# Three chunks per layer of an MLP's second product as seven block products, with groups and chunks strictly alternating

## The chip, the cores and the metric

The kernel runs on one core of a Trainium2 chip. The metric is the device time of one execution in microseconds, taken as the median of several runs. The core's engines are TensorE (PE, with PEld for its weight loads), VectorE (DVE), ScalarE (ACT), GpSimd (POOL) and SyncE (SP, which issues the DMA transfers here).

## The reference

A decoder trunk of two layers over 512 tokens of width 1024. The mixers differ from layer to layer (spatial gating beside latent attention in layer 0, gated linear attention in layer 1); the change touches only the MLP, which is the same in both:

```python
def sqrelu_mlp(x, w1, w2):            # w1: 1024 x 4096, w2: 4096 x 1024, all float32
    return jnp.square(jax.nn.relu(x @ w1)) @ w2
...
        x = layer_norm(ALPHA * x + y, ln1_g[layer], ln1_b[layer])
        x = layer_norm(ALPHA * x + sqrelu_mlp(x, w_ff1[layer], w_ff2[layer]), ln2_g[layer], ln2_b[layer])
```

## The kernel before

**Precision.** Each float32 operand is split in two parts for the matmuls: a high part (`whi`, `hh`), which ACT makes by a cast, and a low part (`wlo`, `hl`), which DVE makes by subtracting the high part from the operand. A product is then three matmuls: high by high, low by high, high by low. So a weight piece of 128 x 1024 costs one DMA, one ACT cast and one DVE subtraction (`split`, lines 164 and 165).

**First product, by groups.** `ff` cuts the 4096 hidden columns into eight groups. Group g holds 256 columns from each half of the hidden dimension. Its operands are cut in 2 x 2 blocks: the transposed x into A11 to A22 (halves of the model dimension by halves of the tokens), w1 into B11 to B22, and the hidden result into the blocks C11, C12, C21, C22 (the first index is the token half, the second the hidden half). Group 0 multiplies the blocks plainly, in eight products. Groups 1 to 7 use seven: P1, P2, p3 to p7, whose operands are sums of blocks (s1 to s4 of x, kept for the whole layer, and t1 to t4 of w1, made on DVE by `sum1`, line 374). `product` runs the 24 matmuls of one product and then, by `step`, the DVE work for which it completes the inputs: V after p6, X after p5 and V, C22 after X and p7, C12 after p3, C11 after P2, C21 after p4. The list LATER sets the order of the seven. Each finished hidden block goes through `relu2`: ACT relu, ACT square, ACT cast to `hh`; the subtraction that makes `hl` is put on the list `late` and issued on DVE by the next `flush`, which stands ahead of each product.

**Second product, by chunks.** Chunk c multiplies the hidden blocks of group c by the rows of w2 that belong to them. In `ff2_half` one token tile t (128 tokens) and one half n of the 1024 output columns make a bank of 12 matmuls of 512 columns, after which DVE adds the bank onto XN (`add_half`, line 208). A chunk is eight such halves, 96 matmuls. Chunks 6 and 7 are multiplied together at the end, where the layer norm follows.

**Order.** `slots` lists products and halves in PE's order and `wseq` the weight pieces in the order of their use. Ahead of each slot `upto(n)` issues the loads of pieces up to six places beyond n, and the casts, sums and subtractions of the pieces up to n; for a group's product n grows with the group's number (three places ahead in group 1, six from group 4 on). PE and DVE run the MLP in the order in which the code issues. The slots of before are group 0, chunk 0, group 1, chunk 1, group 2, chunk 2, groups 3 and 4, chunk 3, group 5, chunk 4, group 6, chunk 5, group 7, chunks 6 and 7.

**Buffers.** Raw w2 pieces go round three buffers (tag `raw`), high and low parts of weights round eight each, hidden parts `hh` and `hl` round eight each. The PSUM banks of both products are dealt in turn from six.

## Time and profile before

| | |
|---|---|
| time, median of 3 runs | 1167.64 us (1166.27 to 1169.44) |
| the profiled execution | 1168.8 us, of which the trace spans 1167.1 us |
| PE, DVE, ACT busy | 98%, 71%, 44% of the span |
| mean granted TensorE clock | 0.997 |
| traffic | 111.68 MB by DMA, mean 96 GB/s |

An engine's busy share counts the time in which at least one of its instructions ran. A matmul's record is longer than the distance to the next matmul's start, since they are pipelined; the same holds to a lesser degree on DVE and ACT. For what a stretch costs, distances between starts are therefore read. [...]

### The profile page before, as it was taken

To read this page: it belongs to the slowest core of one execution; us is meant where nothing else is said; L and a number is where in the kernel's file an instruction comes from. 1 tells how busy PE (TensorE), PEld (TensorE's weight loads), DVE (VectorE), ACT (ScalarE), POOL (GpSimd) and SP (SyncE) were. 2 spreads that over 40 slices of the span, in tenths; PEclk is the share of its full clock that TensorE was granted. 3 is DMA by queue.
4 is the path that set the end of the run, shared out by engine and by line. 5 is a ranking of instruction groups with operands and counts; after the bars stand their busy time and mean duration, and the time that the engine had idled before them with its cause. 6 is when DMAs were issued, how large, how long until landed. Compare 5 with 4: busy or idle time off the path is not lost.

```text
span 1167.1 us, 17136 instructions
## 1 busy us (share of the span) xinstructions
PE 1142.6 (98%) x6888; PEld 996.6 (85%) x6888; DVE 827.2 (71%) x1562; ACT 516.1 (44%) x801; POOL 5.0 (0%) x13
## 2 busy tenths in 40 slices
PE   8999999999999999999999999999999999999997
PEld 8988788898889998998888888778997899889986
DVE  6745687786766767657758559898767577676655
ACT  5467462444343634533254433443544437345330
POOL 0000000000000000000000000000000000000000
PEclk9999999999999999999999999999999999999999
DMA  7413143133412342224235312212133224314121
GB/s 254 140 37 108 55 132 104 37 109 109 126 57 88 127 126 74 89 74 140 72 98 145 90 55 73 73 61 67 59 125 117 85 85 144 127 38 127 54 90 55
DMA packets 84207, 111.68 MB, mean 96 GB/s; under 512 B 6080, under 2 KB 53056, under 8 KB 84128
## 3 DMA queue, kind: packets, MB, share of 16 engines
q1 hardware_dynamic: 84128, 110.59, 30.1%
q8 instruction: 54, 0.88, 0.3%
q14 instruction: 25, 0.20, 0.1%
HBM read 108.47 MB, written 2.10 MB: 95 GB/s over the span
## 4 chain that ended last, share of the span: by engine, by line
PE 88%; DVE 7%; ACT 4%; DMA 0%; issue 0%; SPq 0%; DVEq 0%; ACTq 0%
PE f L451 23%; PE f L161 10%; PE f L159 10%; PE f L160 10%; PE vg L159 3%; PE vg L160 3%; PE vg L161 3%; PE op L159 2%; PE op L161 2%; PE op L160 2%; PE sc L836 1%; PE qk L159 1%; PE qk L160 1%; PE qk L161 1%; PE o L858 1%; PE pl L1117 1%
## 5 line engine op out<-in xcount | busy, mean ns | idle before, releaser
L161 PE MATMUL f<-whi,hl 128*128 128x512 f32 x448 | 178.0, 397 | 5.5 <-DVE hl L431 5.5
L159 PE MATMUL f<-whi,hh 128*128 128x512 f32 x448 | 177.9, 397 | 1.3 <-ACT hh L430 1.3
L164 ACT CAST whi<-cr 128x1024 fp32r<-128x1024 f32 x98 | 100.8, 1048 | 174.7 <-PE f L161 81.4
L160 PE MATMUL f<-wlo,hh 128*128 128x512 f32 x448 | 177.3, 396 | 0.0
L165 DVE TENSOR_TENSOR wlo<-cr,whi 128x1024 fp32r<-128x1024 f32 x98 | 119.2, 1220 | 23.0 <-ACT whi L164 23.0
L451 PE MATMUL f<-XH,wlo 128*128 128x256 f32 x448 | 125.9, 281 | 0.0
L451 PE MATMUL f<-XH,whi 128*128 128x256 f32 x448 | 125.8, 281 | 0.0
L451 PE MATMUL f<-XL,whi 128*128 128x256 f32 x448 | 125.8, 281 | 0.0
L161 PEld LDWEIGHTS f<-whi,hl 128*128 128x128 f32 x448 | 84.7, 189 | 27.8 <-DVE hl L431 8.1
L208 DVE SCALAR_TENSOR_TENSOR XN<-XN,f 128x512 f32<-128x512 f32 (+1 forms) x113 | 74.3, 678 | 43.9 <-PE f L161 43.1
L159 PEld LDWEIGHTS f<-whi,hh 128*128 128x128 f32 x448 | 84.7, 189 | 21.1 <-ACT hh L430 2.1
L160 PEld LDWEIGHTS f<-wlo,hh 128*128 128x128 f32 x448 | 84.8, 189 | 19.3
L451 PE MATMUL f<-sl,whi 128*128 128x256 f32 x336 | 94.5, 281 | 0.0
L451 PE MATMUL f<-sh,wlo 128*128 128x256 f32 x336 | 94.5, 281 | 0.0
L451 PE MATMUL f<-sh,whi 128*128 128x256 f32 x336 | 94.4, 281 | 0.0
L431 DVE TENSOR_TENSOR hl<-r,hh 128x512 fp32r<-128x512 f32 x64 | 44.1, 690 | 60.5 <-ACT hh L430 60.5
L451 PEld LDWEIGHTS f<-XL,whi 128*128 128x128 f32 x448 | 84.4, 188 | 0.5
L451 PEld LDWEIGHTS f<-XH,whi 128*128 128x128 f32 x448 | 84.4, 188 | 0.5
L451 PEld LDWEIGHTS f<-XH,wlo 128*128 128x128 f32 x448 | 84.4, 188 | 0.0
L164 ACT CAST whi<-raw 128x1024 fp32r<-128x1024 f32 x56 | 58.0, 1050 | 54.0 <-PE f L451 35.7
L137 ACT CAST whi<-raw 128x1024 fp32r<-128x1024 f32 (+3 forms) x61 | 60.2, 991 | 47.6 <-DMA raw<-in_w_in_odd 18.8
L138 DVE TENSOR_TENSOR wlo<-raw,whi 128x1024 fp32r<-128x1024 f32 (+3 forms) x61 | 69.7, 1148 | 14.6 <-ACT whi L137 14.3
(270 smaller groups left out, 2528.7 us busy)
## 6 DMA issues: line engine op xcount, KB each, us to landing
raw<-in_w_ff SPq DMA_DIRECT2D x70, 512.0 KB, 4.1
cr<-in_w_ff SPq DMA_DIRECT2D x58, 512.0 KB, 4.0
raw<-in_w_in_odd SPq DMA_DIRECT2D x24, 512.0 KB, 4.0
XN<-in_x SPq DMA_DIRECT2D x16, 256.0 KB, 3.0
raw<-in_w_in_even SPq DMA_DIRECT2D x8, 512.0 KB, 3.8
raw<-in_w_out_even SPq DMA_DIRECT2D x8, 512.0 KB, 3.6
raw<-in_w_out_odd SPq DMA_DIRECT2D x8, 512.0 KB, 3.5
LB<-in_ln_b SPq DMA_DIRECT2D x4, 512.0 KB, 3.8
```

The costliest lines, as they stand in the source:

```text
L137: nc.scalar.copy(hi[:, :n], raw[:, :n])
L138: nc.vector.tensor_tensor(lo[:, :n], raw[:, :n], hi[:, :n].bitcast(F32), ALU.subtract)
L159: nc.tensor.matmul(acc, lh, rh, start=first, stop=False)
L160: nc.tensor.matmul(acc, lh, rl, start=False, stop=False)
L161: nc.tensor.matmul(acc, ll, rh, start=False, stop=last)
L164: nc.scalar.copy(hi, src)
L165: nc.vector.tensor_tensor(lo, src, hi.bitcast(F32), ALU.subtract)
L208: nc.vector.scalar_tensor_tensor(x, x, ALPHA if first else 1.0, acc, ALU.mult, ALU.add)
L431: late.append(lambda: nc.vector.tensor_tensor(f(hl), r, f(hh).bitcast(F32), ALU.subtract))
L451: nc.tensor.matmul(d, l, r, start=first and j == k == i == 0, stop=j == 1 and k == HK_ - 1 and i == 2, skip_group_check=True)
L836: nc.tensor.matmul(sc[:, :N], qts[t][:B_QK, h, :], KT[:, h, :N], start=True, stop=True)
L858: nc.tensor.matmul(os[t][:, h, :], pT[:, j * P:(j + 1) * P], V[:, j, h, :], start=j == 0, stop=j == t)
```

## The change

Chunks 1, 3 and 5 (`SEVEN`) are also multiplied by seven block products. Their hidden blocks are the left operands: C11 serves as A11, C12 as A12, C22 as A22, and s1 to s4 are sums and differences of the four, made on DVE and split like any operand (`h_sums`, in three steps that go out with three consecutive flushes). The weight blocks of w2 (256 rows by 512 columns) give B11, B21, B22 and the sums t1 to t4, made in place in the raw buffers; B21 is loaded a second time for t4. `product2` runs one product, 12 matmuls into two banks, and adds the banks onto XN. P1 and P2 share a pair of banks, so do p5 and p3, and p7 and p4. What p6 and P1 add to several blocks is gathered in V2, over all three chunks, and `add_V2` puts it onto XN once, behind chunk 5. V2 lies in the second halves of LG and LB, so V and X of all groups now lie in the first halves.

Chunks 0, 2 and 4 stay plain; chunks 2 and 4 take the token tiles in the order 2, 3, 0, 1. The groups' order of products is now P1, p5, p7, p6, P2, p4, p3. The slots are group 0, chunk 0, group 1, chunk 1, group 2, chunk 2 and so on to group 5, chunk 5, then groups 6 and 7 and the end.

```diff
+    SEVEN = (1, 3, 5)
...
+            if isinstance(g, tuple):
+                for m in {"B11": ("B11", "B12"), "B21": ("B21",), "t1": ("B22",), "t2": ("B21 again",)}.get(n, ()):
+                    raw = raws[g, m] = wp.tile([P, WG], F32, tag="raw", name="raw", bufs=3)
+                    i, j = BLOCK[m[:3]]
+                    r = i * 2048 + g[1] * GF
+                    nc.sync.dma_start(raw.rearrange("p (k c) -> p k c", k=2),
+                                      w2[r:r + GF, j * 512:(j + 1) * 512].rearrange("(k p) c -> p k c", p=P))
+                return
...
+                if n == "t4" and isinstance(g, tuple):
+                    y = "B21 again"
...
+            if g in SEVEN:
+                hs[g, i, j] = r
+                if (i, j) == (1, 0):
+                    late.append(lambda: h_sums(g))
+                    return
...
+        def h_sums(g):
+            a11, a21, a22 = hs[g, 0, 0], hs[g, 1, 0], hs[g, 1, 1]
+            def cast(n, r):
+                hh, hl = hq[g][n] = term_tiles()
+                nc.scalar.copy(f(hh), r)
+                return lambda: h_lo(hh, hl, r)
+            def first():
+                nc.vector.tensor_tensor(a11, a11, a21, ALU.subtract)
+                nc.vector.tensor_tensor(a21, a22, a21, ALU.subtract)
+                s1, s3 = cast("s1", a21), cast("s3", a11)
+                late.append(lambda: second(s1, s3))
+            def second(s1, s3):
+                nc.vector.tensor_tensor(a22, a11, a22, ALU.add)
+                s2 = cast("s2", a22)
+                s1()
+                s3()
+                late.append(lambda: third(s2))
+            def third(s2):
+                a12 = hs[g, 0, 1]
+                nc.vector.tensor_tensor(a12, a22, a12, ALU.subtract)
+                s4 = cast("s4", a12)
+                s2()
+                late.append(s4)
+            first()
...
-            V = LG[:, g % 2 * 512:(g % 2 + 1) * 512]
-            X = LB[:, g % 2 * 512:(g % 2 + 1) * 512]
+            V, X = LG[:, :512], LB[:, :512]
...
+        TWO = {"P1": "a", "P2": "a", "p5": "d", "p3": "d", "p7": "f", "p4": "f", "p6": "b"}
+        ADDS = {"P2": (0, 0, ALU.add), "p5": (2, 1, ALU.subtract), "p7": (2, 1, ALU.subtract),
+                "p3": (0, 1, ALU.subtract), "p4": (2, 0, ALU.add)}
+        def product2(c, n):
+            g = "w", c
+            op, w = PRODUCTS[n]
+            hh, hl = hq[c][{"A11": (0, 0), "A12": (0, 1), "A22": (1, 1)}.get(op, op)]
+            wh, wl = got_w.pop((g, w))
+            first = (g, TWO[n]) not in banks
+            if first:
+                banks[g, TWO[n]] = [bank("f2") for _ in range(2)]
+            for i, acc in enumerate(banks[g, TWO[n]]):
+                for k in range(2):
+                    for m, (l, r) in enumerate(((hh, wh), (hh, wl), (hl, wh))):
+                        nc.tensor.matmul(acc, l[:, k, tb(i)], r[:, k], start=first and k == m == 0, stop=k == 1 and m == 2,
+                                         skip_group_check=True)
+            for i, acc in enumerate(banks[g, TWO[n]]):
+                if n == "P1" and c == min(SEVEN):
+                    nc.scalar.mul(V2[i], acc, -1.0)
+                elif n in ("P1", "p6"):
+                    nc.vector.tensor_tensor(V2[i], V2[i], acc, ALU.subtract if n == "P1" else ALU.add)
+                else:
+                    t, half, sign = ADDS[n]
+                    x = XN[:, t + i, half * 512:(half + 1) * 512]
+                    nc.vector.tensor_tensor(x, x, acc, sign)
...
-        LATER = ("P1", "p5", "p7", "p6", "p3", "P2", "p4")
+        LATER = ("P1", "p5", "p7", "p6", "P2", "p4", "p3")
+        AGAIN = ("P1", "p5", "P2", "p7", "p6", "p3", "p4")
...
-            wseq.extend((g, n) for n in ("B11", "t1", "t3", "t2", "B22", "B21", "t4"))
+            wseq.extend((g, n) for n in ("B11", "t1", "t3", "t2", "B21", "t4", "B22"))
...
+            if c in SEVEN:
+                slots.extend((("w", c), n) for n in AGAIN)
+                wseq.extend((("w", c), n) for n in ("B11", "B21", "t1", "t3", "t2", "B22", "t4"))
+            else:
+                slots.extend(("w2", c, n, t, i) for n in range(2) for i, t in enumerate((2, 3, 0, 1) if c else range(NT)))
+                wseq.extend(("w2", c, n, h) for n in range(2) for h in range(2))
...
-        mid = NG // 2 - 1
         for c in range(1, NG - 2):
-            for g in (c,) if c < mid else (c, c + 1) if c == mid else (c + 1,):
-                put_group(g)
+            put_group(c)
             put_chunk(c)
+        put_group(NG - 2)
...
+            if isinstance(s[0], tuple):
+                upto(place[s[0], PRODUCTS[s[1]][1]] + TERMS)
+                flush()
+                product2(s[0][1], s[1])
+                if s == (("w", max(SEVEN)), AGAIN[-1]):
+                    add_V2()
```

In the following rows `wlo`, `hl` are low parts, `whi`, `hh` high parts; the numbers are those of buffers.

DVE at the end of group 1 and the start of chunk 1 in layer 0, before: from the step for C22 on (`LB` is X, `LG` is V; `r_3029` is C22, `r_3069` C12, `r_3104` C11, `r_3140` C21; `raw` are pieces of w2 for chunk 1, `cr` of w1 for group 2).

```order
L485 TENSOR_TENSOR r_3029<-LB_73,f1_2971 128x512
L165 TENSOR_TENSOR wlo_3037<-raw_2829,whi_3036 128x1024
L431 TENSOR_TENSOR hl_3032<-r_3029,hh_3031 128x512
L489 TENSOR_TENSOR f1_3041<-LB_73,f1_3041 128x512
L165 TENSOR_TENSOR wlo_3074<-raw_2864,whi_3073 128x1024
L431 TENSOR_TENSOR hl_3068<-r_3069,hh_3067 128x512
L165 TENSOR_TENSOR wlo_3109<-raw_2925,whi_3108 128x1024
L431 TENSOR_TENSOR hl_3103<-r_3104,hh_3102 128x512
L493 TENSOR_TENSOR f1_2971<-f1_2971,LG_72 128x512
L165 TENSOR_TENSOR wlo_3146<-cr_2927,whi_3145 128x1024
L431 TENSOR_TENSOR hl_3139<-r_3140,hh_3138 128x512
L208 SCALAR_TENSOR_TENSOR XN_71<-XN_71,f2_3150 128x512
```

The same place in the changed kernel, from the sum t1 of chunk 1 to the low part of s1 (`raw_2829` holds B11, then t1, then t2; `raw_2831` holds B12, then t3; `raw_2927` is B22; `r_3065` is C11, then s3; `r_3101` is C21, then s1; `r_3025` is C22, then s2; `r_3146` is C12).

```order
L385 TENSOR_TENSOR raw_2829<-raw_2829,raw_2831 128x1024
L385 TENSOR_TENSOR raw_2831<-raw_2831,raw_2927 128x1024
L165 TENSOR_TENSOR wlo_3109<-raw_2829,whi_3108 128x1024
L469 TENSOR_TENSOR r_3065<-r_3065,r_3101 128x512
L470 TENSOR_TENSOR r_3101<-r_3025,r_3101 128x512
L545 TENSOR_TENSOR f1_3120<-LB_73,f1_3120 128x512
L385 TENSOR_TENSOR raw_2829<-raw_2829,raw_2927 128x1024
L165 TENSOR_TENSOR wlo_3155<-raw_2831,whi_3154 128x1024
L165 TENSOR_TENSOR wlo_3159<-raw_2829,whi_3158 128x1024
L165 TENSOR_TENSOR wlo_3163<-raw_2927,whi_3162 128x1024
L475 TENSOR_TENSOR r_3025<-r_3065,r_3025 128x512
L444 TENSOR_TENSOR hl_3115<-r_3101,hh_3114 128x512
```

Where four low parts of weights, four of hidden blocks and three steps stood between the end of p7 and the first addition of the chunk, there are now three weight sums, more low parts and three sums of hidden blocks ahead of the low part of s1 (last row), which the second product of the chunk reads.

ACT at the same place, before: from the cast of a piece of chunk 1 to the cast of C21.

```order
L164 CAST whi_3167<-raw_2964 128x1024
L428 ACTIVATE r_3140<-f1_2971 128x512
L429 ACTIVATE r_3140<-r_3140 128x512
L430 CAST hh_3138<-r_3140 128x512
L164 CAST whi_3172<-cr_2927 128x1024
L164 CAST whi_3195<-cr_2929 128x1024
L164 CAST whi_3199<-cr_2927 128x1024
L164 CAST whi_3249<-cr2_2996 128x1024
```

And in the changed kernel, from C21's relu to the square of C12 (the two rows `LG_72<-f2`, `LB_73<-f2` copy the banks of P1 into V2; `whi_3154` is t3's high part, `hh_3114` that of s1, `hh_3117` that of s3).

```order
L448 ACTIVATE r_3101<-f1_2969 128x512
L449 ACTIVATE r_3101<-r_3101 128x512
L164 CAST whi_3108<-raw_2829 128x1024
L581 ACTIVATE LG_72<-f2_3173 128x512
L581 ACTIVATE LB_73<-f2_3174 128x512
L164 CAST whi_3154<-raw_2831 128x1024
L465 CAST hh_3114<-r_3101 128x512
L465 CAST hh_3117<-r_3065 128x512
L448 ACTIVATE r_3146<-f1_3120 128x512
L449 ACTIVATE r_3146<-r_3146 128x512
```

Between C21's square and the high part of s1 there now stand two weight casts and two copies that wait for product P1 of the chunk.

SP, which issues the loads, before: from the second piece of chunk 1 on.

```order
L403 DMA raw_2864<-in_w_ff2 128x2x512
L367 DMA cr2_2477<-in_w_ff1 128x4x256 x2
L403 DMA raw_2925<-in_w_ff2 128x2x512
L367 DMA cr_2927<-in_w_ff1 128x4x256
L367 DMA cr2_2996<-in_w_ff1 128x4x256
L367 DMA cr_2929<-in_w_ff1 128x4x256
L367 DMA cr2_2996<-in_w_ff1 128x4x256
L403 DMA raw_2964<-in_w_ff2 128x2x512
L403 DMA raw_3164<-in_w_ff2 128x2x512
```

And in the changed kernel, from B12 of chunk 1 (`raw_2831`) on; `raw_2866` is B21, `raw_2927` B22, `raw_2963` B21 again.

```order
L363 DMA raw_2831<-in_w_ff2 128x2x512
L376 DMA cr2_2477<-in_w_ff1 128x4x256 x2
L363 DMA raw_2866<-in_w_ff2 128x2x512
L376 DMA cr_3032<-in_w_ff1 128x4x256
L376 DMA cr_3034<-in_w_ff1 128x4x256
L376 DMA cr2_3104<-in_w_ff1 128x4x256 x2
L363 DMA raw_2927<-in_w_ff2 128x2x512
L363 DMA raw_2963<-in_w_ff2 128x2x512
L417 DMA raw_3235<-in_w_ff2 128x2x512
```

B22 and the second B21 now stand behind the four loads of group 2, at the place where one piece of chunk 1 and one of chunk 2 stood.

## Rows read from the trace of the kernel before

**Rows 1.** The page, part 1: busy time, share of the span, instructions

```profile
PE 1142.6 (98%) x6888; PEld 996.6 (85%) x6888; DVE 827.2 (71%) x1562; ACT 516.1 (44%) x801; POOL 5.0 (0%) x13
```

**Rows 2.** The page, part 4: the chain that ended last, shares by engine

```profile
PE 88%; DVE 7%; ACT 4%; DMA 0%; issue 0%; SPq 0%; DVEq 0%; ACTq 0%
```

**Rows 3.** Windows: pairs 1 and 2, the rest, chunk 3, group 5; layer 1

```profile
core 0: us, PE busy (x) PEld busy (x) DVE busy (x) ACT busy (x) POOL busy (x), PEclk, DMA share, GB/s
269.85:314.00 44.15, 42.73 (x266) 37.95 (x264) 32.23 (x36) 19.46 (x25) 0.00 (x0) 1.00 0.34 107
314.00:359.76 45.76, 44.29 (x265) 39.09 (x264) 28.20 (x33) 18.72 (x24) 0.00 (x0) 0.96 0.29 93
359.76:526.14 166.38, 166.38 (x1129) 153.71 (x1128) 114.65 (x129) 81.03 (x107) 0.00 (x0) 1.00 0.31 99
399.55:421.86 22.31, 22.31 (x99) 18.09 (x97) 17.51 (x21) 10.74 (x15) 0.00 (x0) 1.00 0.20 61
421.86:441.75 19.89, 19.89 (x170) 19.89 (x168) 12.84 (x15) 10.45 (x15) 0.00 (x0) 1.00 0.45 145
858.85:902.99 44.14, 42.72 (x265) 37.95 (x264) 32.23 (x36) 19.46 (x25) 0.00 (x0) 1.00 0.34 107
902.99:947.56 44.57, 42.74 (x266) 37.96 (x265) 28.09 (x33) 18.73 (x24) 0.00 (x0) 1.00 0.30 95
947.56:1113.93 166.37, 166.37 (x1129) 153.70 (x1128) 114.65 (x129) 81.05 (x107) 0.00 (x0) 1.00 0.31 99
```

**Rows 4.** Timeline of PE, start of chunk 2, layer 0: start, duration, idle, releaser

```profile
334.32 0.51 PE L159 MATMUL f<-whi,hh 128*128 128x512 f32 x1 [0.27 <-ACT hh L430]
...
336.26 0.65 PE L161 MATMUL f<-whi,hl 128*128 128x512 f32 x1 [1.21 <-DVE hl L431]
```

**Rows 5.** Windows behind that start

```profile
336.47:339.88 3.41, 3.41 (x9) 2.63 (x9) 1.04 (x2) 1.84 (x3) 0.00 (x0) 0.50 0.00 0
339.88:343.30 3.42, 3.42 (x17) 2.77 (x16) 2.86 (x3) 1.00 (x1) 0.00 (x0) 1.00 0.02 5
```

**Rows 6.** Timeline of DVE from the end of p6, group 2, layer 0

```profile
325.63 0.69 DVE L497 TENSOR_TENSOR LG<-f,LG 128x512 f32<-128x512 f32 x1 [8.19 <-PE f L451]
326.36 0.69 DVE L498 TENSOR_TENSOR LB<-LG,f 128x512 f32<-128x512 f32 x1
327.08 0.69 DVE L485 TENSOR_TENSOR r<-LB,f 128x512 f32<-128x512 f32 x1
327.69 1.22 DVE L165 TENSOR_TENSOR wlo<-raw,whi 128x1024 fp32r<-128x1024 f32 x1
329.78 0.69 DVE L431 TENSOR_TENSOR hl<-r,hh 128x512 fp32r<-128x512 f32 x1 [0.88 <-ACT hh L430]
```

**Rows 7.** Timeline of DVE: weight-sized operations in a row, and two additions

```profile
341.04 1.22 DVE L374 TENSOR_TENSOR cr<-cr 128x1024 f32<-128x1024 f32 x1
342.18 1.22 DVE L165 TENSOR_TENSOR wlo<-raw,whi 128x1024 fp32r<-128x1024 f32 x1
343.31 1.22 DVE L374 TENSOR_TENSOR cr<-cr,cr 128x1024 f32<-128x1024 f32 x1
...
448.34 1.28 DVE L208 SCALAR_TENSOR_TENSOR XN<-XN,f 128x512 f32<-128x512 f32 x2
449.54 1.22 DVE L374 TENSOR_TENSOR cr<-cr,cr 128x1024 f32<-128x1024 f32 x1
```

**Rows 8.** Timeline of ACT at the same group end

```profile
325.49 1.05 ACT L164 CAST whi<-raw 128x1024 fp32r<-128x1024 f32 x1 [1.80 <-PE f L451]
327.80 0.63 ACT L428 ACTIVATE r<-r 128x512 f32<-128x512 f32 x1 [1.26 <-DVE r L485]
328.46 0.63 ACT L429 ACTIVATE r<-r 128x512 f32<-128x512 f32 x1
...
331.11 1.09 ACT L428 ACTIVATE r<-f 128x512 f32<-128x512 f32 x2 [1.36 <-DVE f L489]
```

**Rows 9.** The page, part 6: loads of MLP weights, median us to landing

```profile
raw<-in_w_ff SPq DMA_DIRECT2D x70, 512.0 KB, 4.1
```

More of the change, by code (lines that the diff above doesn't have):

```diff
@@ L396, in terms1 @@
                 split(hi, lo, raw)
+                if isinstance(g, tuple):
+                    got_w[g, n] = [z.rearrange("p (k c) -> p k c", k=2) for z in (hi, lo)]
+                    return
                 his, los = ([z.rearrange("p (k c) -> p k c", k=HK_)[:, :, tb(j)] for j in range(2)] for z in (hi, lo))
@@ L419, in scratch, with term_tiles @@
         def scratch(g):
-            return fp.tile([P, S], F32, name="r", **({"tag": "x", "bufs": 4} if g and next(turns) == "x" else {"tag": "q"}))
+            x = g in SEVEN or g and next(turns) == "x"
+            return fp.tile([P, S], F32, name="r", **({"tag": "x", "bufs": 4} if x else {"tag": "q"}))
+        f = lambda z: z.rearrange("p j t -> p (j t)")
+        def term_tiles():
+            return hp.tile([P, 2, HALF_S], F32R, tag="hh", name="hh"), hp.tile([P, 2, HALF_S], F32R, tag="hl", name="hl")
@@ L431, in relu2 @@
-            late.append(lambda: nc.vector.tensor_tensor(f(hl), r, f(hh).bitcast(F32), ALU.subtract))
-            hq[g][i, j] = hh, hl
-        late = []
+            if g in SEVEN:
+                hs[g, i, j] = r
+                if (i, j) == (1, 0):
+                    late.append(lambda: h_sums(g))
+                    return
+            hh, hl = hq[g][i, j] = term_tiles()
+            nc.scalar.copy(f(hh), r)
+            late.append(lambda: h_lo(hh, hl, r))
+        def h_sums(g):
[22 more added lines that the diff above has]
+            first()
@@ L437, in flush @@
+        late, hs = [], {}
         def flush():
-            while late:
-                late.pop(0)()
+            now, late[:] = late[:], []
+            for step in now:
+                step()
         banks, state = {}, {}
@@ L502, in product, with add_V2 @@
             step("C21", {"V", "C22", "p4"}, c21)
+        V2 = [z[:, 512:] for z in (LG, LB)]
+        TWO = {"P1": "a", "P2": "a", "p5": "d", "p3": "d", "p7": "f", "p4": "f", "p6": "b"}
[23 more added lines that the diff above has]
+                    nc.vector.tensor_tensor(x, x, acc, sign)
+        def add_V2():
+            for t, half, sign in ((0, 1, ALU.add), (2, 1, ALU.add), (2, 0, ALU.subtract)):
+                for i in range(2):
+                    x = XN[:, t + i, half * 512:(half + 1) * 512]
+                    nc.vector.tensor_tensor(x, x, V2[i], sign)
         def ff2_half(c, n, t):
@@ L518, in put_group @@
             slots.extend((g, n) for n in LATER)
-            wseq.extend((g, n) for n in ("B11", "t1", "t3", "t2", "B22", "B21", "t4"))
+            wseq.extend((g, n) for n in ("B11", "t1", "t3", "t2", "B21", "t4", "B22"))
         def put_chunk(c):
-            slots.extend(("w2", c, n, t) for n in range(2) for t in range(NT))
-            wseq.extend(("w2", c, n, h) for n in range(2) for h in range(2))
+            if c in SEVEN:
[4 more added lines that the diff above has]
+                wseq.extend(("w2", c, n, h) for n in range(2) for h in range(2))
         wseq += [(0, n) for n in ("B11", "B21", "B12", "B22")]
         put_chunk(0)
-        mid = NG // 2 - 1
         for c in range(1, NG - 2):
-            for g in (c,) if c < mid else (c, c + 1) if c == mid else (c + 1,):
-                put_group(g)
+            put_group(c)
             put_chunk(c)
+        put_group(NG - 2)
         put_group(NG - 1)
@@ L535, in ff @@
         for i, w in enumerate(wseq):
-            if w[0] != "w2" and w[1] == "B11" and i and wseq[i - 1][0] == "w2":
+            if w[1] == "B11" and i and not isinstance(w[0], tuple) and not isinstance(wseq[i - 1][0], int):
                 wseq[i - 1:i + 1] = wseq[i - 1:i + 1][::-1]
@@ L580, in ff @@
                 else:
-                    upto(min(need + 1 + TERMS, need + 1 + 2 * (s[3] + 1)))
+                    upto(min(need + 1 + TERMS, need + 1 + 2 * (s[4] + 1)))
                 flush()
                 ff2_half(s[1], s[2], s[3])
+                continue
+            if isinstance(s[0], tuple):
[4 more added lines that the diff above has]
+                    add_V2()
                 continue
```

5 lines of the change are left out of this document (2 added, 3 removed).

## The prediction

> **What bounds the kernel now.** I read the busy table first: TensorE (PE) is busy for 98% of the span, VectorE (DVE) for 71% and ScalarE (ACT) for 44% [rows 1]; PE work makes up 88% of the chain that ended last [rows 2]. So the time is PE's work plus what PE waits, and the change has to be judged on both. The stretches of one layer's MLP come next [rows 3]. The reader should see three things there. A chunk of the second product is 96 matmuls of 512 columns in 22.31 us, 0.232 us each by start to start (the 397 ns of a record overlap its neighbours). A group of the first product is 168 matmuls in 19.89 us, so one of its seven products takes 2.84 us. And the first two group-and-chunk pairs of a layer take 44.1 to 45.8 us where 42.2 is all PE work, while the rest of the layer (five groups, three chunks) takes 166.4 us, exactly 5 x 19.89 + 3 x 22.31.
>
> The pairs that run over are those whose chunk follows its own group directly: PE idles 0.27 and 1.21 us for the high and low part of a hidden block [rows 4]. [...] Later chunks of before have a group between, and wait for nothing. The change takes that distance away everywhere.
>
> Last I read DVE's order of time at the end of a group [rows 6]: it idles 8.19 us for the end of product p6, though work for later products stands behind in its queue, and then works through. So its list counts from p6's end.
>
> **Prices.** A weight-sized operation (128x1024, sum or low part) starts 1.135 us after the one before [rows 7]; a half-sized one (128x512) 0.60, from PSUM too, and 0.72 when it reads the result of the one before [rows 6, 7]. A square or cast behind its predecessor on ACT comes after 0.66 us, independent ones after about 0.5; a weight cast takes 1.05 [rows 8]. A load of 512 KB lands 4.1 us after issue [rows 9].
>
> **What the change removes.** Seven products of 12 matmuls for eight: 12 x 0.232 = 2.79 us a chunk, for six chunks 16.7 us of PE.
>
> **What it adds.** Per seven-product chunk DVE gets four weight sums, three more low parts, four sums of hidden blocks, three more of their low parts, and 14 additions for 8 (two of them on ACT in the first). That is 7 x 1.135 + 13 x 0.60 = 15.7 us more. A pair had 28.1 to 32.2 us of DVE in 44 to 46 [rows 3]; with it DVE has at least the 39.4 us (42.2 - 2.8) that PE keeps. What decides is where the work stands in the queue. The second product, p5, needs s1, which is made of C21 and C22. C21 is ready only after p4, the last but one product of the group.
>
> *Third chunk (the fifth alike), zero at the end of p6.* PE finishes P2, p4, p3 and the chunk's P1 at 2.84, 5.68, 8.52 and 11.3. DVE's queue: V, X, C22 (2.1); sums t1, t3 (4.4); the low part of t1 waits until 5.2, since ACT has relu and square of C22 and C11 ahead of its cast, and ends at 6.4; low part of C22, sum t2, low parts of t3 and C11 (9.8); C21 (10.5, though its bank is full at 5.68); low part of t2 (11.7). Sums s3, s1 wait to 12.6, because ACT casts B22 and the next group's B11 before C21's relu and square, and end at 13.9; C12, low part of B22, sum s2 (16.3); low part of s1: 16.9. So p5 starts at 16.9, 5.6 us late. Then low parts of s3 and C12 and two additions of P1 (19.3), four weight-sized pieces (23.9), sum s4 and low part of s2 (25.1), additions of p5, low part of s4, additions of P2: 28.1. Product p6 takes the two PSUM banks that P2 leaves (six banks go round, a chunk takes eight), so it starts at 28.1 where p7 ends at 16.9 + 8.4 = 25.3: 2.8 us more. p6, p3, p4 end at 36.5; the next group's first product needs the bank of p3's first addition, DVE's next 5 x 1.135 + 5 x 0.60 = 8.7 us, at 36.8. The chunk takes 36.8 - 8.5 = 28.3 us for 22.3, the pair 48.2 for 42.2.
>
> *First chunk.* Weight pieces are split fewer places ahead in group 1, so B11 and B21 too come after V. 2.1; low part of B11 3.2; C22's waits on ACT until 5.4, 6.0; B21's 7.2; C11's 7.8; C21 8.5; sum t1 9.6. Sum t3 waits for B22: with three raw buffers its load can only go into B21's, free at 7.2, and lands at 11.3 (12.5). Low part of t1, s3, s1 (15.0); C12, sum t2, low part of t3 (17.9); the low parts of t2 and B22 wait for casts that ACT has behind the two copies of P1, s1, s3 and C12 (19.6, 21.1); s2, low part of s1: 22.3. p5 is 11.0 late. By the same list P2's additions are done at 32.3, p6 waits 1.6, and the next group starts at 41.0: the chunk takes 32.5, the pair 52.4 us for 44.1. The second load of B21, into t3's buffer at 17.9, lands at 22.0 and DVE asks at 23.5: hidden.
>
> *Plain chunks 2 and 4* now follow their own groups and begin with the token tiles of C21. By the same list C21's high part is there 1.8 us after the group's end in chunk 2, its low part costs 0.2 more: 44.2 us the pair, for 45.8 and 44.6. In chunk 4 DVE is five places ahead with weights, which puts t1 and t2 sums and low parts between: 4.1 us, 46.3 for 42.2. Groups 6 and 7 together stay 39.8; the six additions of the running sum (3.6 us) make V of group 6 some 1.9 us late and its p4 1.2.
>
> **Sum.** A layer: 52.4 + 44.2 + 48.2 + 46.3 + 48.2 + 39.8 + 1.2 = 280.3 us, for 256.3 and 255.1, the three stretches of each layer added up [rows 3]: +24.0 and +25.2. The profiled execution's own 1168.8 us becomes 1218; it stands 1.2 above the median, so 1217.
>
> **A rule beside the row.** DVE's idle 8.19 us with work behind it [rows 6] shows that nothing passes a waiting instruction. [...] If entries could pass one another, most of the waits inside the lists would vanish and the time would come near the second rival's 1183.
>
> **Rivals.** (1) *All hidden, faster.* Weights are split places ahead and the group's first four products leave DVE idle [rows 6], so only PE's 16.7 us count, and at most the 9.8 us of boundary waits that the early pairs have over 42.2 go too: 1142 to 1152. It holds from the point where s1's low part is done by 11.3; the pure work before it is 9 x 1.135 + 3 x 0.72 + 8 x 0.60 = 17.2 in the first chunk and 14.9 in the third, and V cannot start earlier. Chance 5%. (2) *Queues without waits*: ACT's casts and the load come in time, only DVE's work counts. P2's additions at 27.1 and 26.0, chunks of 27.0 and 25.9, plain pairs at 42.2: +6.4 and +7.6 a layer, 1183. ACT's part against it: even in before DVE waits 0.88 us for a high part [rows 6]. Chance 15%. (3) *The clock.* The waits are longer than those that had the half clock behind them [rows 4, 5], and a stretch as there costs 1.7 us. Behind p5's wait most of that is covered, since p6 waits for additions anyway (0.8 in chunk 1); behind p6's 1.3 shows, and in chunks 2 and 4 all of it: 3 x 1.3 + 0.8 + 2 x 1.7 = 8 a layer, 1234. [...] The trace agrees in one of the four early pairs alone, the others keep 1.00 [rows 3], so I leave it out of the likeliest sum. Chance 15%.
>
> **Numbers.** Forecast 60%, rivals 5, 15 and 15%, something worse (a late load before a head of DVE's queue) 5%. The range 1182 to 1240 reaches to rivals 2 and 3. The runs of before spread 0.27%, so 0.3% is about what can be told from no change: faster 4%, same 2%, slower 94%.
>
> **What would show it.** PE idle before p5's low-part matmul, about 11 us in the first and 5 to 6 us in the third and fifth chunk, released by DVE; 1 to 3 us before p6; pairs near 52, 44, 48, 46, 48; DVE near-continuously busy from p6's end to the next group's. Pairs under 42 would show rival 1, a granted clock of 0.50 in most chunks rival 3. I would be wrong most easily in ACT's part, which is counted entry by entry from one pattern.

## The result: 1254.55 us, slower, and the profile after

| | before | after |
|---|---|---|
| time, median of 4 runs each | 1167.72 us | 1254.55 us (1254.04 to 1255.65) |
| ratio, 95% interval | | 1.0741 (1.0727 to 1.0755) |
| the profiled execution, its span | 1168.8, 1167.1 us | 1255.65, 1253.8 us |
| mean granted clock | 0.997 | 0.963 |

The forecast was 1217 us, at most 1240: the sign was right, the size was not, +87 us for +49. The page after, part 1 (busy) and part 4 (shares of the chain), to be read beside [rows 1, 2]:

```profile
PE 1157.9 (92%) x6816; PEld 1002.5 (80%) x6816; DVE 927.0 (74%) x1690; ACT 544.1 (43%) x841; POOL 4.5 (0%) x13
PE 72%; DVE 14%; ACT 8%; DMA 5%; issue 2%; SPq 0%; DVEq 0%; ACTq 0%
```

PE has 72 matmuls fewer and yet 15.3 us more busy time. The matmuls taken away are worth 16.7 us, so the others took some 32 us longer; 88.8 us of the two layers ran at the half clock (granted clock 0.50). Its idle time grew from 1167.1 - 1142.6 = 24.5 us to 95.9. So -16.7 + 32 + 71.4 = 86.7 us, the whole difference of the spans. Windows by stretch, to be read beside [rows 3]; layer 0, pairs 1 to 5, then groups 6 and 7:

```profile
269.98:321.34 51.36, 41.90 (x253) 37.02 (x252) 42.45 (x49) 23.87 (x32) 0.00 (x0) 0.90 0.29 93
321.34:369.04 47.70, 43.86 (x266) 39.05 (x265) 32.55 (x38) 20.39 (x26) 0.00 (x0) 0.96 0.32 103
369.04:416.26 47.22, 43.04 (x254) 37.37 (x253) 39.06 (x48) 21.00 (x28) 0.00 (x0) 0.93 0.26 84
416.26:466.86 50.60, 44.83 (x265) 39.74 (x264) 33.06 (x39) 20.28 (x26) 0.00 (x0) 0.93 0.32 100
466.86:511.85 44.99, 40.43 (x254) 35.39 (x252) 39.25 (x48) 21.25 (x28) 0.00 (x0) 1.00 0.27 88
511.85:561.72 49.87, 42.79 (x337) 42.59 (x336) 36.70 (x43) 25.43 (x35) 0.00 (x0) 0.90 0.25 80
```

Layer 1 has the same stretches within 0.3 us. The close (chunks 6 and 7, first 168 matmuls) of layer 1, first before, then after:

```profile
1113.93:1153.24 39.31, 38.99 (x170) 31.46 (x169) 25.43 (x52) 6.68 (x12) 0.00 (x0) 1.00 0.17 60
```

```profile
1193.31:1239.85 46.54, 41.91 (x171) 33.27 (x169) 27.32 (x54) 8.00 (x13) 0.00 (x0) 0.93 0.16 57
```

Every stretch is over, not the seven-product pairs alone: pairs 2 and 4, groups 6 and 7 and the close hold no product that the change added. PE's longest waits in layer 0 (timeline of PE; in brackets the idle time and what ended it):

```profile
296.45 0.50 PE L577 MATMUL f<-whi,hh 128*128 128x512 f32 x1 [3.64 <-ACT hh L465]
303.00 0.80 PE L577 MATMUL f<-whi,hl 128*128 128x512 f32 x1 [5.82 <-DVE hl L444]
345.23 0.80 PE L159 MATMUL f<-whi,hh 128*128 128x512 f32 x1 [3.84 <-ACT hh L456]
442.07 0.80 PE L159 MATMUL f<-whi,hh 128*128 128x512 f32 x1 [5.77 <-ACT hh L456]
503.40 0.47 PE L577 MATMUL f<-whi,hh 128*128 128x512 f32 x1 [3.04 <-DVE XN L587]
533.28 0.58 PE L508 MATMUL f<-XH,whi 128*128 128x256 f32 x1 [7.08 <-DVE r L541]
571.33 0.79 PE L159 MATMUL f<-whi,hh 128*128 128x512 f32 x1 [4.67 <-ACT hh L456]
```

The first two stand before p5 of chunk 1, with s1's high and low part; the fifth is p6 of chunk 5, behind P2's additions. These are the forecast's. The other four are the starts of chunks 2 and 4, p4 of group 6 and the close. Three places show where they come from.

*Chunk 2.* DVE subtracts a w2 piece, SP then issues the next load into that raw buffer, ACT waits for it, and C22's relu stands behind that cast. DVE's rows are the subtraction, the step for C22 and the step for C21, with whose tokens the chunk begins. Timelines of DVE, SP and ACT:

```profile
329.43 1.22 DVE L165 TENSOR_TENSOR wlo<-raw,whi 128x1024 fp32r<-128x1024 f32 x1
...
334.36 0.69 DVE L541 TENSOR_TENSOR r<-LB,f 128x512 f32<-128x512 f32 x1
...
342.55 0.69 DVE L549 TENSOR_TENSOR f<-f,LG 128x512 f32<-128x512 f32 x1
```

```profile
330.67 0.37 SPq L417 DMA_DIRECT2D raw<-in_w_ff  x1
```

```profile
336.56 1.05 ACT L164 CAST whi<-raw 128x1024 fp32r<-128x1024 f32 x1 [5.52 <-DMA raw<-in_w_ff]
337.51 0.63 ACT L448 ACTIVATE r<-r 128x512 f32<-128x512 f32 x1
```

C22 is ready at 335.05, ACT takes it at 337.51. So its low part comes late on DVE (340.20), and C21's step, which stands behind that, begins at 342.55, where p4, the sixth product, ended at about 338.4 (six times 2.84 us after 321.34). The load was issued 0.02 us after DVE was done with the buffer, and DVE was late there because it was still at chunk 1's work: that chunk's last additions began at 327.10. In chunk 4 ACT waits 5.50 us for a load in the same place.

*Group 6.* Timeline of DVE: the first of the six additions of V2 (line 593; the last begins at 520.77), a sum that waits for its load, and V:

```profile
517.76 0.68 DVE L593 TENSOR_TENSOR XN<-XN,LG 128x512 f32<-128x512 f32 x1
...
526.43 1.22 DVE L385 TENSOR_TENSOR cr<-cr,cr 128x1024 f32<-128x1024 f32 x1 [1.44 <-DMA cr<-in_w_ff]
...
531.10 0.68 DVE L553 TENSOR_TENSOR LG<-f,LG 128x512 f32<-128x512 f32 x1
```

Between the additions and V stand seven weight-sized operations (521.38 to 531.10). p4 needs the bank that the step for C22 reads (532.54), so PE waits until 533.28.

*Close.* p3 ends group 7 at 561.72, but DVE comes to C12's step only at 568.60, and C12's high part reaches PE at 571.33. Timeline of ACT, a cast that waits for its load and then C22's square; timeline of DVE, C22's low part and C12's step, with two w2 pieces and other work between:

```profile
557.89 1.05 ACT L164 CAST ws<-raw 128x1024 fp32r<-128x1024 f32 x1 [1.70 <-DMA raw<-in_w_ff]
558.85 0.62 ACT L449 ACTIVATE r<-r 128x512 f32<-128x512 f32 x1
```

```profile
560.50 0.69 DVE L444 TENSOR_TENSOR hl<-r,hh 128x512 fp32r<-128x512 f32 x1 [3.83 <-ACT hh L456]
...
568.60 0.69 DVE L545 TENSOR_TENSOR f<-LB,f 128x512 f32<-128x512 f32 x1
```

### The profile page after: what moved, and what is told of

Its sections match the earlier page's. It is cut to its first block, busy times and chain, and to the rows that moved or that the text cites. A ratio compares the mean times of both kernels' runs of the same rounds, so it can differ in the third digit from the quotient of the medians.

```text
span 1253.8 us, 17198 instructions
## 1 busy us (share of the span) xinstructions
PE 1157.9 (92%) x6816; PEld 1002.5 (80%) x6816; DVE 927.0 (74%) x1690; ACT 544.1 (43%) x841; POOL 4.5 (0%) x13
## 4 chain that ended last, share of the span: by engine, by line
PE 72%; DVE 14%; ACT 8%; DMA 5%; issue 2%; SPq 0%; DVEq 0%; ACTq 0%
PE f L508 14%; PE f L159 6%; PE f L160 6%; PE f L577 6%; PE f L161 6%; DVE wlo L165 4%; DMA raw<-in_w_ff 3%; PE vg L159 3%; PE vg L160 2%; PE vg L161 2%; PE op L159 2%; PE op L161 2%; PE op L160 2%; ACT whi L164 2%; ACT r L449 1%
## 5 line engine op out<-in xcount | busy, mean ns | idle before, releaser
L165 DVE TENSOR_TENSOR wlo<-cr,whi 128x1024 fp32r<-128x1024 f32 x98 | 118.9, 1218 | 18.7 <-ACT whi L164 18.6
L164 ACT CAST whi<-raw 128x1024 fp32r<-128x1024 f32 x74 | 76.1, 1048 | 73.7 <-DMA raw<-in_w_ff 26.4
L160 PE MATMUL f<-wlo,hh 128*128 128x512 f32 x256 | 104.7, 409 | 0.0
L444 DVE TENSOR_TENSOR hl<-r,hh 128x512 fp32r<-128x512 f32 x82 | 55.5, 687 | 59.8 <-ACT hh L456 59.8
L165 DVE TENSOR_TENSOR wlo<-raw,whi 128x1024 fp32r<-128x1024 f32 x74 | 89.4, 1218 | 5.8 <-ACT whi L164 5.8
L508 PEld LDWEIGHTS f<-XL,whi 128*128 128x128 f32 x448 | 86.7, 193 | 0.5
L577 PE MATMUL f<-whi,hl 128*128 128x512 f32 x168 | 71.3, 425 | 16.6 <-DVE hl L444 16.6
L508 PEld LDWEIGHTS f<-XH,wlo 128*128 128x128 f32 x448 | 86.7, 193 | 0.0
L159 PEld LDWEIGHTS f<-whi,hh 128*128 128x128 f32 x256 | 50.8, 198 | 40.9 <-ACT hh L456 30.0
L208 DVE SCALAR_TENSOR_TENSOR XN<-XN,f 128x512 f32<-128x512 f32 (+1 forms) x65 | 43.4, 675 | 51.4 <-PE f L161 51.3
```

The source lines that it names most:

```text
L159: nc.tensor.matmul(acc, lh, rh, start=first, stop=False)
L160: nc.tensor.matmul(acc, lh, rl, start=False, stop=False)
L164: nc.scalar.copy(hi, src)
L165: nc.vector.tensor_tensor(lo, src, hi.bitcast(F32), ALU.subtract)
L208: nc.vector.scalar_tensor_tensor(x, x, ALPHA if first else 1.0, acc, ALU.mult, ALU.add)
L444: nc.vector.tensor_tensor(f(hl), r, f(hh).bitcast(F32), ALU.subtract)
```

## The experiments

Ratios are to the kernel before, run on the same chip; spans in brackets are 95% intervals. "After" is the changed kernel.

**Order alone, and distance alone.** The first kernel has the changed kernel's order (of groups and chunks, of products and of token tiles) and no seven-product chunk; the second is the kernel before with the early pairs one group ahead too.

```diff
-    SEVEN = (1, 3, 5)
+    SEVEN = ()
```

> The changed kernel's order of groups, chunks and products, but all chunks plain (no chunk uses seven products). If the lost distance between a group and its chunk is what costs (theory 1), every pair 1 to 5 waits like the plain pairs 2 and 4 of the changed kernel (47.7 and 50.6 us) and the close waits too: per layer about 5 x 48 - 216.5 + 7 = 30 more than before, 1229 us, in any case over 1200. If the added DVE work of the seven products is what costs and plain chunks only inherit its lag (theory 2), the pairs go back to 42 to 45 us: under 1182 us.

```diff
-        mid = NG // 2 - 1
+        mid = 1
```

> The kernel before with one number changed, so that group 2 already comes ahead of chunk 1 and every chunk has a foreign group between its own group and itself. Theory 1: the waits of the first two pairs (9.8 us over both layers, with the half clock behind one of them) go: 1157 to 1160 us. If those waits have another cause (the work of the first groups on DVE), the time stays at 1166 to 1169.

Measured: 1211.43 us, 1.0365 (1.0348 to 1.0383), and 1159.59 us, 0.9924 (0.9910 to 0.9939). Windows of pair 4 with order alone, and of a pair of the second kernel:

```profile
405.44:452.97 47.53, 44.03 (x265) 39.19 (x264) 28.46 (x33) 18.81 (x24) 0.00 (x0) 0.96 0.27 89
```

```profile
353.42:395.61 42.19, 42.19 (x266) 38.00 (x265) 30.53 (x35) 18.77 (x25) 0.00 (x0) 1.00 0.32 100
```

Half of the loss, 43 us, is the new order with no seven-product chunk at all: each chunk start waits 1.56 to 3.51 us for a hidden high part, and the close takes 46.6 us. One group of distance, with the products' old order, leaves pairs of 42.2 us throughout, and gives the fastest kernel of this study. The two kernels differ in the order of products too. What that order does can be seen in pairs 1 and 2, which have no distance in the kernel before either: 44.15 and 45.76 us there [rows 3], 45.84 and 44.28 with order alone. So these pairs lose by distance, and hardly by the products' order. The other half, 43 us, comes with the seven products.

**Work for VectorE.** The next kernel is after, whose products take plain hidden blocks in place of s1 to s4 (the sums of hidden blocks are left out).

```diff
-                if (i, j) == (1, 0):
-                    late.append(lambda: h_sums(g))
-                    return
...
-            hh, hl = hq[c][{"A11": (0, 0), "A12": (0, 1), "A22": (1, 1)}.get(op, op)]
+            hh, hl = hq[c][{"A11": (0, 0), "A12": (0, 1), "A22": (1, 1), "s1": (1, 1), "s2": (1, 1), "s3": (0, 0), "s4": (0, 1)}[op]]
```

> The changed kernel, but the products of chunks 1, 3 and 5 take plain hidden blocks where s1 to s4 belong, so that no sums of hidden blocks are made (that part of the computation is changed). If the place of s1 in the queues is what delays (theory 1), the waits before p5 go (9.5, 3.5 and 1.5 us a layer) with the half clock behind them: about 15 + 4 a layer, 1217 us, and pair 1 falls under 45. If DVE's total work bounds the pairs (theory 2), they fall by what DVE is spared, 7 x 0.60 = 4.2 us each: 1229 us, and waits remain, moved to p6 and to the next group.

Measured: 1236.54 us, 1.0576 (1.0558 to 1.0594), 18 us less. Pair 5 takes 42.63 us; the window of pair 1:

```profile
271.57:318.14 46.57, 41.79 (x253) 36.39 (x252) 37.84 (x41) 22.12 (x29) 0.00 (x0) 0.96 0.31 99
```

Without p5's dependence on C21 the pairs still don't come down to 39.4 us: new waits stand at P2 and p6 for additions (2.33 and 1.15 us in chunk 3), and pair 4 and group 6 lose as much as in after. VectorE's remaining work took part of the place. This run takes away both work of VectorE and the place of s1 in the queues, so it doesn't tell the two apart.

The weight sums of the seven-product chunks were then given to GpSimd (twelve a layer; the expectation's "eighteen" is a slip):

```diff
-                nc.vector.tensor_tensor(raws[g, n], raws[g, x], raws[g, y], ALU.add)
+                eng = nc.gpsimd if isinstance(g, tuple) else nc.vector
+                eng.tensor_tensor(raws[g, n], raws[g, x], raws[g, y], ALU.add)
```

> The changed kernel, with the eighteen weight sums per layer of the seven-product chunks and their groups that belong to the chunks (four in each of three chunks) done by GpSimd and not by VectorE. If VectorE's queue is what makes p5 and p6 wait in chunks 1, 3 and 5 (theory: load of VectorE), its 4 x 1.14 us a chunk leave the queue, and pairs 1, 3 and 5 fall by 3 to 5 us each: 24 us in all, about 1230 us. Rival: GpSimd takes much longer than 1.14 us for the same addition, and the wait for the sum takes the place of the wait for the queue: 1250 us or above. A second rival, that these waits come from the order alone and not from VectorE's work, gives no change, 1254 us.

Measured: 1263.77 us, 1.0820 (1.0801 to 1.0840), 9 us more than after. By the time the first rival holds, but the wait for the sums is not all of it. The page's part 1, then timelines of POOL and of DVE beside it, twice:

```profile
PE 1161.2 (92%) x6816; PEld 1004.6 (80%) x6816; DVE 925.2 (73%) x1666; ACT 544.1 (43%) x841; POOL 62.4 (5%) x37
```

```profile
374.06 2.40 POOL L386 TENSOR_TENSOR raw<-raw 128x1024 f32<-128x1024 f32 x1 [67.57 <-DVE wlo L165]
381.22 2.39 POOL L386 TENSOR_TENSOR raw<-raw 128x1024 f32<-128x1024 f32 x1 [4.76 <-DMA raw<-in_w_ff]
```

```profile
374.49 3.04 DVE L165 TENSOR_TENSOR wlo<-raw,whi 128x1024 fp32r<-128x1024 f32 x1 [0.57 <-ACT whi L164]
382.12 0.69 DVE L554 TENSOR_TENSOR LG<-f,LG 128x512 f32<-128x512 f32 x1 [4.58 <-PE f L509]
```

An addition takes 2.40 us there for 1.22 on DVE, 1.97 times as long. The low part of weights that begins during the first of these additions takes 3.04 us for 1.22, while V, which begins during the second and reads a PSUM bank, keeps its 0.69. VectorE, with 24 operations of 1.22 us fewer than in after, is busy for 925.2 us where it was 927.0: of the 29.3 us taken off its queue all but 1.8 came back as longer operations. This run shows that, and is no test of a lighter load on VectorE.

**The clock.** Dummy matmuls into an unused bank were put into after's long waits, so that PE is not idle there.

```diff
+        SPIN = {(1, "p5"): 36, (3, "p5"): 12, (5, "p5"): 4, (5, "p6"): 11, (2, 0): 14, (4, 0): 22, (6, "p4"): 28, "close": 18}
...
+            if (c, n) in SPIN:
+                spin(SPIN[c, n])
```

> The changed kernel with extra matmuls into an unused PSUM bank ahead of the products that wait, a little less work than each wait is long (36, 12, 4, 11, 14, 22, 28, 18 matmuls of 512 columns at eight places a layer), so that PE does not idle there. If the half clock behind the waits costs by itself, the granted clock goes to about 1.00 and the time falls by much of the 32 us that PE is busy longer than its matmuls account for: 1225 to 1240 us. If the half-clock stretches lie under waits that would be there anyway, the time stays at 1254, within 3 us.

Measured: 1244.17 us, 1.0650 (1.0633 to 1.0668), mean clock 0.996. Windows: the stretch behind chunk 1's wait in after, and chunk 2 with the dummies; then PE before p6 of chunks 1 and 3, with the dummies.

```profile
297.11:307.35 10.24, 4.42 (x11) 3.47 (x11) 9.53 (x11) 5.95 (x8) 0.00 (x0) 0.50 0.39 129
```

```profile
345.13:367.81 22.68, 22.68 (x97) 18.11 (x97) 17.20 (x20) 8.05 (x9) 0.00 (x0) 1.00 0.22 69
```

```profile
312.25 0.47 PE L586 MATMUL f<-whi,hh 128*128 128x512 f32 x1 [1.41 <-DVE XN L596]
...
406.60 0.47 PE L586 MATMUL f<-whi,hh 128*128 128x512 f32 x1 [2.58 <-DVE XN L596]
```

Of the 32 us that PE's matmuls took longer only 10 come back. Chunks 2 and 4 of layer 0 fall by 1.1 and 2.1 us, the close of layer 1 by 2.4; the seven-product chunks stay (31.15 us for 31.47 in chunk 1), since PE there waits for DVE whether its matmuls are fast or slow: DVE is busy for 9.53 of the 10.24 us in the first window, PE for 4.42. What the half clock took there comes back as the wait before p6. In every place but one (chunk 4 of layer 0) PE still waits 0.4 to 2.0 us behind the dummies, so it is not the dummies that hold it.

**The three places without an added product.** Each was mended by itself: V2's additions behind P1 of group 7; weight pieces at most three places ahead in the groups that no seven-product chunk follows; group 7's products in the order of before.

```diff
-                if s == (("w", max(SEVEN)), AGAIN[-1]):
-                    add_V2()
...
+            if s == (NG - 1, "P1"):
+                add_V2()
```

> The changed kernel with the six additions of the running sum V2 behind product P1 of group 7 instead of behind chunk 5. Ahead of p4 of group 6 PE waits 7.1 us for DVE's step C22, with 6.8 to 10.2 us of half clock around it. If the six additions (3.6 us) make DVE late, that wait falls to about 3.5 us: 4 to 6 us a layer, 1243 to 1247. If the weights of group 7, which stand ahead of V too, set it alone, the time stays at 1254.

```diff
-            upto(place[s[0], PRODUCTS[s[1]][1]] + 1 + min(TERMS, 2 + s[0]))
+            upto(place[s[0], PRODUCTS[s[1]][1]] + 1 + (min(TERMS, 2 + s[0]) if s[0] in SEVEN else 3))
```

> The changed kernel with weights split three places ahead (instead of four to six) in groups 2, 4, 6 and 7. If ACT's queue is what holds back C22's relu there (a cast of a weight piece that has not landed stands ahead of it) and weights of later pieces ahead of C21 on DVE, the waits of 3.8 us (chunk 2), 5.8 (chunk 4), 4.7 (close) go to about 1.5 to 2 each and that in group 6 from 7.1 to about 3: some 13 us a layer, 1228. If the chain p4, C21, relu, square, cast by itself sets these waits, they stay and the time with them (1250 to 1256).

```diff
-            slots.extend((g, n) for n in LATER)
-            wseq.extend((g, n) for n in ("B11", "t1", "t3", "t2", "B21", "t4", "B22"))
+            old = g == NG - 1
+            slots.extend((g, n) for n in (("P1", "p5", "p7", "p6", "p3", "P2", "p4") if old else LATER))
+            wseq.extend((g, n) for n in ("B11", "t1", "t3", "t2", *(("B22", "B21", "t4") if old else ("B21", "t4", "B22"))))
```

> The changed kernel with the products of group 7 alone in the order of before (p3, P2, p4 last). The wait of 4.7 us inside the close is for C12, which p3 now gives last. If that order is its cause, the wait falls under 1 us and the half clock behind it goes too: 5 to 7 us a layer, 1241 to 1245. If ACT's casts that wait for loads set it, whatever the order, the time stays within 2 us of 1254.

Measured: 1249.44 us, 1.0690 (1.0667 to 1.0713); 1227.71 us, 1.0508 (1.0488 to 1.0528); 1241.31 us, 1.0620 (1.0600 to 1.0640). With the second, chunks 2 and 4 wait 1.56 us, which with order alone only chunk 2 did (chunk 4: 3.50), and groups 6 and 7 take 41.30 us; but the close waits 7.62 us for a hidden low part, which stands on DVE behind pieces of w2 whose loads now come later. With the third the close is that of before, to the hundredth. Window of groups 6 and 7 with the second, then window of the close in layer 1 with the third:

```profile
503.06:544.36 41.30, 40.02 (x338) 39.84 (x337) 35.93 (x44) 24.17 (x34) 0.00 (x0) 1.00 0.19 62
```

```profile
1186.72:1226.03 39.31, 38.99 (x170) 31.47 (x169) 25.53 (x52) 6.68 (x12) 0.00 (x0) 1.00 0.18 63
```

The first took the wait in group 6 from 7.08 us to 2.07 in layer 0 and from 7.21 to 3.67 in layer 1, and made one of 1.67 and 1.74 in group 7. The three together (six places kept in group 7, because of that close):

```diff
+            upto(place[s[0], PRODUCTS[s[1]][1]] + 1 + (min(TERMS, 2 + s[0]) if s[0] in SEVEN or s[0] == NG - 1 else 3))
```

> The changed kernel with three edits together: weight pieces at most three places ahead in groups 2, 4 and 6; the products of group 7 in the order they had before the change; and the additions of V2 behind P1 of group 7. Alone the first gave 26.8 us (though with three places in group 7 too, and a new wait of 8 us in the close), the second 13.2, the third 5.1. If these are separate places with prices that add up, 1254.5 - 26.8 - 13.2 - 5.1 = 1209 us, with a close of 39.3 us and no wait over 3 us in chunks 2 and 4 and group 6. Rival: the waits move on to the next reader in VectorE's queue, as in the runs before, and the three together give less than 35 us, 1220 us or above.

Measured: 1224.80 us, 1.0492 (1.0474 to 1.0509), 30 us less than after and not 45. The prices don't add up. Pairs 2 and 4 keep their gain (44.29 us both), but in group 7 V's step now stands behind the six additions of V2, and p4 waits 4.08 us; and the close, with six places kept, takes 43.06 us in layer 1 and not 39.3. PE in group 7:

```profile
545.87 0.55 PE L508 MATMUL f<-XH,whi 128*128 128x256 f32 x1 [4.08 <-DVE r L541]
```

**Seven products with a group of distance.** Each seven-product chunk stands one group later. The sums of its hidden blocks and part of their splits are made during that group, the other splits between the chunk's own products. V2's additions stand behind P2 of group 7, and the orders of products and token tiles are those of before.

```diff
+        put_group(1)
         for c in range(1, NG - 2):
-            put_group(c)
+            put_group(c + 1)
             put_chunk(c)
-        put_group(NG - 2)
...
+            if s[0] - 1 in SEVEN and s[1] in ("P1", "p5", "p7", "p6"):
+                if s[1] == "P1":
+                    steps[s[0] - 1] = h_steps(s[0] - 1)
+                next(steps[s[0] - 1])
```

> Chunks 1, 3 and 5 by seven products as in the changed kernel, but each chunk has the next group ahead of it, and the sums of hidden blocks and their parts are made while that group runs (eight high and low parts suffice, since they are made shortly before use). The DVE work is the same as in the changed kernel. If distance is what the changed kernel lacks (theory 1), PE's 16.7 us are saved against the run with all chunks ahead (1159.6): 1143 to 1150 us. If DVE's total work is too much for seven products (theory 2), DVE lags and the time is 1160 or more, with waits in the pairs 1, 3 and 5.

Measured: 1207.70 us, 1.0338 (1.0321 to 1.0356). The plain pairs are clean (42.2 us), the seven-product chunks take 27.97 to 29.13 us, where the plain ones take 22.3: so the lost distance alone does not account for the whole. Against the second kernel of this study, with the same distance and no seven-product chunk, the difference is 48 us. The six chunks have 37 of these. Some 12 are in the two closes, where PE waits 4.84 and 4.71 us for a low part that stands behind the six additions of V2 (541.37 to 545.06 in layer 0). Two runs ask what holds these chunks. In the first their weight sums are left out; in the second P2 stands one product later.

```diff
-                nc.vector.tensor_tensor(raws[g, n], raws[g, x], raws[g, y], ALU.add)
+                if not isinstance(g, tuple):
+                    nc.vector.tensor_tensor(raws[g, n], raws[g, x], raws[g, y], ALU.add)
```

> The kernel with the seven-product chunks one group ahead (1207.7 us), and the four weight sums of each such chunk left out (the products take the summands as they are, so this part of the computation is missing). Its seven-product chunks took 29.1, 28.0 and 28.7 us, with VectorE busy for 28.2 of the 29.1 us of the first. If VectorE's amount of work bounds them, each falls by its 4 x 1.14 us, to 24 or 25 us: six times 4.5 is 27, about 1181 us. Rival: what bounds them is the dependence of P2 on the reading of P1's bank, the product p5 apart; then VectorE's work doesn't matter, and the time stays within 5 us of 1207.

```diff
-        AGAIN = ("P1", "p5", "P2", "p7", "p6", "p3", "p4")
+        AGAIN = ("P1", "p5", "p7", "P2", "p6", "p3", "p4")
```

> The kernel with the seven-product chunks one group ahead (1207.7 us), with product P2 behind p7 in each of those chunks and not before it: two products and not one lie between P1 and P2, which share a bank that VectorE or ScalarE must have read. Four of its six seven-product chunks wait 3.97 us at P2. If the distance from P1 to P2 is what costs, these four waits go and nothing comes for them: 16 us less, about 1192 us. Rival: VectorE's amount of work bounds these chunks; then the wait shows up one or two products later, at p6 or p3, and the time stays within 4 us of 1207.

Measured: 1185.92 us, 1.0161 (1.0146 to 1.0176), 22 us less; and 1232.87 us, 1.0563 (1.0547 to 1.0578), 25 us more. Windows of chunk 1 with distance, and of the same with the sums left out, then PE's longest waits in chunk 1 with distance and with P2 behind p7 (3.62 us with the sums left out); last, with distance, a window of chunk 3, DVE ahead of P2 there, and PE at P2:

```profile
308.58:337.71 29.13, 22.58 (x87) 17.62 (x85) 28.21 (x34) 17.79 (x25) 0.00 (x0) 0.88 0.28 92
```

```profile
311.12:336.43 25.31, 21.36 (x87) 16.48 (x85) 23.00 (x29) 14.71 (x22) 0.00 (x0) 0.93 0.33 106
```

```profile
326.72 0.77 PE L572 MATMUL f<-whi,hh 128*128 128x512 f32 x1 [6.35 <-DVE XN L582]
```

```profile
331.69 0.76 PE L572 MATMUL f<-whi,hh 128*128 128x512 f32 x1 [8.81 <-DVE XN L582]
```

```profile
399.79:427.79 28.00, 22.29 (x87) 16.60 (x86) 23.94 (x31) 13.93 (x20) 0.00 (x0) 0.94 0.28 93
```

```profile
408.81 0.69 DVE L444 TENSOR_TENSOR hl<-r,hh 128x512 fp32r<-128x512 f32 x1 [2.03 <-ACT hh L454]
409.42 0.68 DVE L578 TENSOR_TENSOR LG<-LG,f 128x512 f32<-128x512 f32 x1
```

```profile
410.16 0.51 PE L572 MATMUL f<-whi,hh 128*128 128x512 f32 x1 [3.97 <-DVE LG L578]
```

With the sums left out the chunks take 23.8 to 25.3 us, 3.4 to 4.5 less each, close to their 4 x 1.14 us of DVE time: what stands on VectorE is the larger part. In chunk 1 it is the amount, since DVE is busy for 28.21 of 29.13 us. In chunks 3 and 5 it is the place in the queue as well: DVE is busy for only 23.9 to 24.6 of 28.0 to 28.7 us, and P2's wait of 3.97 us ends with the reading of P1's banks, which stands behind a low part for which DVE idles 2.03 us. With the sums left out this wait is 1.52 us. For P2 both expectations fell. The wait at P2 went from 3.97 to 0.97 us, but p6, which takes the two banks that P2 leaves, now has no product between itself and P2, and its wait for P2's additions grew to 8.8 us in every such chunk. In the ring of six banks, more distance for one read of DVE is less for another.

## Why the prediction was wrong

Per layer the forecast was +24.0 and +25.2 us. Layer 0 by its own steps, the close from layer 1:

| stretch | before [rows 3] | forecast | measured | missed by |
|---|---|---|---|---|
| pair 1 | 44.2 | 52.4 | 51.36 | -1.0 |
| pair 2 | 45.8 | 44.2 | 47.70 | +3.5 |
| pair 3 | 42.2 | 48.2 | 47.22 | -1.0 |
| pair 4 | 42.2 | 46.3 | 50.60 | +4.3 |
| pair 5 | 42.2 | 48.2 | 44.99 | -3.2 |
| groups 6 and 7 | 39.8 | 41.0 | 49.87 | +8.9 |
| close | 39.3 | 39.3 | 46.54 | +7.2 |

That is 18.7 us a layer, 37.4 in both: the whole gap from 1217 to 1254.

- **What bounds it, and the direction: right.** Distance before the chunk, and VectorE's queue with it, decide. The two runs on order and distance show the first (+43 and -9 us), the runs with less DVE work the second (-18 and -22 us).
- **Pairs 1 and 3: right within 1.0 us**, with the waits named: p5 is 3.64 + 5.82 = 9.5 us late for 11.0 in chunk 1, 0.72 + 1.90 + 1.55 = 4.2 for 5.6 in chunk 3 (the 0.72 stands before P1's low part). p6's wait is not there in chunks 1 and 3 of layer 0 (1.6 and 2.8 were forecast), because 10.24 and 6.83 us of these chunks ran at the half clock; with the dummies it is there, 1.41 and 2.58 us, and the chunks take the same time. So the terms were right for the full clock, and that their sum held at the half clock too is partly luck.
- **"The fifth alike": the step was wrong.** Group 5 splits its weights one place further ahead than group 3, so DVE makes t1 and t3 at 472.01 and 475.71, ahead of V (478.43), where in group 3 they stand behind V (380.67, then 382.72). p5 waits 1.10 + 0.42 us. Only p6's wait is as forecast (3.04 for 2.8).
- **"By the same list" for chunks 2 and 4: mis-sized terms, 3.84 and 5.77 us for 1.8 + 0.2 and 4.1.** The list took the weights' loads as landed. They are not: DVE, late from the seven-product chunk, hands its raw buffer back late. With plain chunks only, chunk 4 waits 3.50 and chunk 2 1.56, near the list; with pieces three places ahead both wait 1.56. These waits are some half of the two misses; the other half is mostly the half clock behind them (the chunks take 23.80 and 24.79 us for 22.31, with the dummies 22.68 both). The prediction had named ACT's part as its weakest, and it is on ACT that the loads come in.
- **Groups 6 and 7, "1.2": a mis-sized term, 10.1.** The list had the six additions of V2 (3.6 us) and not that DVE comes to them late and that seven weight-sized operations, one waiting 1.44 us for its load, stand between them and V. Moving the additions gave 5 us in both layers together; pieces at most three places ahead left 1.5 of the 10.1.
- **The close: left out of the sum, 7.2 us a layer.** LATER puts p3 last, so C12 is the last block of group 7, and the close begins with its tokens. The change wrote this order for the groups ahead of a seven-product chunk, and group 7 has none behind it. The old order for group 7 alone gives 39.31 us again.
- **The clock (rival 3): real, and not the main cause.** The sum had it at nothing; 10 of the 37 us come back when it is kept up. Rival 3's 17 us at 15% were nearer to that than the zero of the sum. The half-clock stretches are 44.4 us a layer and cost 5 of them net; the seven-product chunks lose next to nothing by them (chunk 1 takes 31.47 us, and 31.15 with the dummies), since PE waits for DVE there in any case.
- **Queues in order: as the lists had them, in the places read here.** On ACT C22's relu stood for 2.46 us behind a cast that had no data (335.05 to 337.51); on DVE V of group 6, whose last product is the fourth (523.2, four times 2.84 us after 511.85), began at 531.10 behind weight sums and low parts.
- **VectorE's added work: right.** 827.2 to 927.0 us busy, 99.8 / 6 = 16.6 us a chunk for 15.7; V2's additions, which the forecast counts in group 6 (3.6 us a layer), are 1.2 of that.

The rivals of 1183 us (queues without waits) and 1142 to 1152 us (all hidden) both fell; even with a group of distance the time was 1207.70. What stays open is how much of the 1.5 to 3.0 us that those chunks take over the plain ones without the weight sums is the ring of banks and how much ACT's part; more banks were not tried. Nor was the order of DVE's queue in the chunks with distance: a reading of P1's banks ahead of the low part that waits.
